# Split FFN and output weights kept in DRAM for the second half of the tokens, with a six-tile chunk between the halves

## The chip, the cores and the metric

The kernel runs on one core of one Trainium2 chip. The metric is the device time of one execution in microseconds: the median of three runs. The core has five engines that work side by side, each through its own list of instructions in order: TensorE (PE) for matmuls, VectorE (DVE), ScalarE (ACT), GpSimd (POOL) and SyncE (SP). SyncE and GpSimd issue DMAs here.

## The reference

Two layers of a trunk on 1152 tokens (1024 of a sample, 128 of a prompt) of width 1024. Each layer is a normalization, an input projection, four mixers, an output projection `w_out` with a gated residual, and then a SwiGLU feed-forward network (FFN) of width 2816 with a gated residual:

```
h = rmsnorm(x) * (1 + scale) + shift
x = x + gate * ((silu(h @ w1) * (h @ w3)) @ w2)
```

All inputs and outputs are float32. The change touches `w_out`, `w1`, `w3` and the order of the FFN.

## The kernel before

A float32 matmul is done as three matmuls of a reduced float32 type: each operand is split into a high part (a rounded copy) and a low part (what is left), and high x high, high x low and low x high are summed in PSUM (`mm3`). Splitting a weight costs one cast on ScalarE and one subtract on VectorE (`wsplit` for `w_out` and `w2`, `wstr` for `w1` and `w3`). Split weights stand in two pools of buffers: the tag `ws` with two buffers, and a pool of 19 large buffers that also holds the activations; raw weights of `wsplit` have one buffer (`wr`).

The tokens are worked on in two halves of 576, each as two quarters of 288. The input side of the FFN, per tile of 128 hidden columns of `w1` and `w3` (22 tiles, index `f`), uses a scheme of seven products in place of eight: `wstr` forms seven split combinations of the four 128x512 pieces of the raw weights (7 casts, 7 subtracts and 4 adds or subtracts of raw pieces), in four buffers; the products are 12 matmuls each, 84 a tile, and VectorE and ScalarE add them up and apply the silu (`ffn_in`). The output side (`ffn_out`) multiplies the hidden tiles of a chunk by `w2`, 48 matmuls a hidden tile and half. Chunks are 2, 4, 4, 4, 4, 4 hidden tiles: an input stage of so many tiles, then an output stage, whose results are added to `x` at once (line 1569, `resid`).

The order of the instructions is written out by generators. `fill_add` queues items, each a pair of `pre` (load and split the weights) and `run` (the matmuls, with a yield after each product). `pre` of the next item is issued after the first yield of the current one. Each layer runs `out_half` (the output projection, eight items for each half), then for both halves all chunks. Beside it `prep(l, 0)` and `prep(l, 1)` make the normalized input of either half (seven buffers `A`) on VectorE and ScalarE; that of half 1 needs the buffers of half 0 and runs around the last output stage of half 0. In layer 0 a generator `side` computes the modulation of layer 1 on VectorE from 24 loads of 1 MB (`wm`, issued by SyncE), stepped three times per hidden tile in both halves.

All weight loads are issued by SyncE, in program order: a load that waits for its buffer holds back those behind it.

Of the kernel before, what the change touches and what calls it, by code (L numbers as in the profile page):

```python
# [21 lines left out]
KT = 8  # L22
# [8 lines left out]
CHUNKS = (2, 4, 4, 4, 4, 4)  # L31
# [249 lines left out]
class Trunk:  # L281
# [10 lines left out]

    SUM = staticmethod(lambda nc: nc.vector)
# [1358 lines left out]
    def layer(s, l, st):  # L1652
# [115 lines left out]
        for p in range(2):  # L1768
            t0 = 0
            sc = []  # L1770
            for ci, nh in enumerate(CHUNKS):
                last = ci == len(CHUNKS) - 1
# [7 lines left out]
        e = len(CHUNKS) - 1  # L1780
# [18 lines left out]
    def out_half(s, l, m, h, mh, ev):  # L1799

        def pre():
# [16 lines left out]
    def wstr(s, l, f):  # L1818

        nc = s.nc  # L1820
        r = s.d("raw")[:, :2048].rearrange("p (x h n) -> p x h n", x=2, h=2)
# [4 lines left out]
        tile_ = [s.d2("ws", F32R, w=1024) if i % 2 else s.t("ws", (128, 2, 1024), F32R, bufs=s.b_ws) for i in range(4)]  # L1826
        B = [None] * 7

        def add(out, a, b, op):
            s.SUM(nc).tensor_tensor(out=out, in0=a, in1=b, op=op)  # L1830

        def part(i, at, src):
            t = tile_[at // 2][:, at % 2]
            hi, lo = t[:, :512], t[:, 512:]
            nc.scalar.copy(hi, src)  # L1835
            nc.vector.tensor_tensor(out=lo, in0=src, in1=hi.bitcast(F32), op=ALU.subtract)  # L1836
            B[i] = (hi, lo)
        part(0, 0, b11)
        add(t3, b22, b12, ALU.subtract)
        add(b12, b12, b11, ALU.subtract)  # L1840
        part(2, 2, b12)
        add(b12, b12, b22, ALU.subtract)
        part(1, 1, b12)
        part(3, 3, b21)
        part(4, 4, t3)
        part(5, 5, b22)
        add(b21, b21, b12, ALU.add)
        part(6, 6, b21)
        return B

    def ffn_in(s, l, p, f, A, hid, sc, side):
# [3 lines left out]
        def pre():  # L1855
            return s.wstr(l, f)

        def run(B):
# [19 lines left out]
            def add(out, a, b, e=nc.vector):  # L1878
                e.tensor_tensor(out=out, in0=a, in1=b, op=ALU.add)  # L1879
# [11 lines left out]
            next(side, None)  # L1891
            nc.scalar.copy(p5, prod(2, "m"))
# [4 lines left out]
            next(side, None)  # L1897
            add(c21, prod(4, "m"), c12)
            add(c22, c21, p5, s.SUM(nc))
            add(c12, c12, p5, s.SUM(nc))  # L1900
# [3 lines left out]
            yield 1580  # L1904
# [214 lines left out]
```

## Time and profile before

| | us |
|---|---|
| median of three runs | 3399.97 |
| lowest and highest | 3396.93, 3400.04 |
| the profiled execution, its own time | 3406.3 |
| its span in the trace | 3404.5 |
| TensorE busy | 3222.8 (95%) |
| VectorE busy | 2613.6 (77%) |
| ScalarE busy | 1436.5 (42%) |
| GpSimd busy | 27.9 (1%) |

The profile is of one execution. Busy time is the time in which an engine had an instruction in work; a share of the span is a mean over stages that differ. The mean granted clock of TensorE over the span is 0.974 of full speed. "Idle before" an instruction, with an arrow to a name, is the time its engine stood still and what ended that. Matmuls are pipelined, so their modelled ends overlap the next by a little.

### The profile page before, as it was taken

Reading aid. Unit: us, or ns where it says so; the run is one execution under the profiler, and the core shown is the slowest. Engines: PE = TensorE matmul, PEld = TensorE weight load, DVE = VectorE, ACT = ScalarE, POOL = GpSimd, SP = SyncE. Lnnn points to the kernel's source line nnn. Section 1 sums busy time; section 2 is a strip of 40 time slices with the busy share of each in tenths; the row PEclk is TensorE's granted clock in tenths of the full one; section 3 lists DMA queues with packets and bytes.
Section 4 is the critical chain, followed back from the end, with each engine's and each line's share of the span. In section 5 each row is a group of like instructions: output and inputs, shape, how many; then the busy total and the mean of one; then the engine's idle time right before and its main releaser. Section 6 shows DMA issues by size and latency. Waiting matters only on the chain. (4 is left out here: it accounts for less than half of the span.)

```text
span 3404.5 us, 64037 instructions
## 1 busy us (share of the span) xinstructions
PE 3222.8 (95%) x26412; PEld 2961.8 (87%) x26412; DVE 2613.6 (77%) x5458; ACT 1436.5 (42%) x2737; POOL 27.9 (1%) x101
## 2 busy tenths in 40 slices
PE   7999999999899999799999999999989999889998
PEld 3657878899889999699998887889889999889998
DVE  6735876558789999999988687655778877988877
ACT  5437254333433443434444635433344434534433
POOL 0000000000000000000000000000000000000000
PEclk8999999999999999899999999999999999989999
DMA  7441101233233333233323110113322232222322
GB/s 275 174 152 31 50 16 34 67 123 132 81 113 124 113 129 100 81 116 121 124 80 107 33 50 17 33 67 127 134 81 82 94 100 81 72 93 94 100 81 72
DMA packets 103889, 319.26 MB, mean 94 GB/s; under 512 B 16496, under 2 KB 33766, under 8 KB 91821
## 3 DMA queue, kind: packets, MB, share of 16 engines
q1 hardware_dynamic: 101692, 300.82, 26.5%
q0 software_dynamic: 1904, 14.35, 1.2%
q8 instruction: 208, 3.41, 0.4%
q14 instruction: 85, 0.69, 0.1%
HBM read 285.58 MB, written 29.56 MB: 93 GB/s over the span
## 5 line engine op out<-in xcount | busy, mean ns | idle before, releaser
L303 PE MATMUL pm<-u,ws 128*128 128x384 f32 x3456 | 680.4, 348 | 14.3 <-DVE ws L347 5.4
L303 PE MATMUL pm<-A,ws 128*128 128x288 f32 x4224 | 631.4, 299 | 28.9 <-ACT ws L1835 7.8
L303 PEld LDWEIGHTS pm<-u,ws 128*128 128x128 f32 x3456 | 603.2, 191 | 42.8 <-issue 8.5
L303 PEld LDWEIGHTS pm<-A,ws 128*128 128x128 f32 x4224 | 587.3, 191 | 39.5 <-ACT ws L1835 8.6
L303 PE MATMUL ps<-hid,ws 128*128 128x288 f32 x4224 | 584.6, 298 | 14.2 <-DVE sc L1879 6.0
L303 PEld LDWEIGHTS ps<-hid,ws 128*128 128x128 f32 x4224 | 570.0, 190 | 23.7 <-DVE sc L1879 7.3
L303 PE MATMUL ps<-A,ws 128*128 128x288 f32 x3168 | 484.3, 301 | 27.6 <-ACT ws L1835 22.1
L303 PEld LDWEIGHTS ps<-A,ws 128*128 128x128 f32 x3168 | 445.5, 192 | 36.1 <-ACT ws L1835 25.3
L1835 ACT CAST ws<-raw 128x512 fp32r<-128x512 f32 x528 | 318.7, 619 | 335.2 <-DVE raw L1830 159.8
L1836 DVE TENSOR_TENSOR ws<-raw,ws 128x512 fp32r<-128x512 f32 x528 | 353.2, 684 | 21.7 <-ACT ws L1835 20.1
L346 ACT CAST ws<-wr 128x1024 fp32r<-128x1024 f32 (+2 forms) x186 | 187.0, 1005 | 269.7 <-DMA wr<-w 94.2
L347 DVE TENSOR_TENSOR ws<-wr,ws 128x1024 fp32r<-128x1024 f32 (+2 forms) x186 | 216.6, 1165 | 98.9 <-ACT ws L346 97.4
L1569 DVE SCALAR_TENSOR_TENSOR x<-ps,mod,x 128x288 f32<-128x288 f32 (+2 forms) x480 | 206.3, 451 | 81.6 <-PE ps L303 79.7
L303 PE MATMUL pm<-mh,ws 128*128 128x288 f32 x1536 | 218.9, 303 | 17.8 <-DVE x L1569 11.4
L303 PEld LDWEIGHTS pm<-mh,ws 128*128 128x128 f32 x1536 | 211.9, 194 | 22.6 <-issue 12.2
L1830 DVE TENSOR_TENSOR raw<-raw 128x512 f32<-128x512 f32 x264 | 180.7, 684 | 2.6
L475 DVE SCALAR_TENSOR_TENSOR acc<-wm,cT,acc 128x512 f32<-128x512 f32 x168 | 121.2, 743 | 0.0
L303 PEld LDWEIGHTS pm<-ws,u 128*128 128x128 f32 x864 | 107.5, 188 | 9.4 <-issue 3.8
L303 PE MATMUL pm<-ws,u 128*128 128x272 f32 (+1 forms) x864 | 114.9, 289 | 0.5 <-DVE lr L879 0.4
L1884 ACT CAST hid<-sc 128x288 fp32r<-128x288 f32 x176 | 75.2, 432 | 77.9 <-DVE sc L1883 77.2
L749 DVE COPY_PREDICATED DS<-masks,ps 128x320 f32<-128x320 uint8 x192 | 89.1, 477 | 21.6 <-PE ps L303 21.4
L1879 DVE TENSOR_TENSOR sc<-ps,p 128x288 f32<-128x288 f32 x176 | 79.5, 452 | 33.0 <-PE ps L303 27.6
(331 smaller groups left out, 3815.9 us busy)
## 6 DMA issues: line engine op xcount, KB each, us to landing
raw<-w SPq DMA_DIRECT2D x176, 512.0 KB, 4.5
wm<-w_mod SPq DMA_DIRECT2D x48, 1024.0 KB, 6.5
wr<-w SPq DMA_DIRECT2D x80, 512.0 KB, 3.7
wr<-w_in SPq DMA_DIRECT2D x48, 512.0 KB, 3.5
wr<-w_out SPq DMA_DIRECT2D x32, 512.0 KB, 3.6
dft<-dft_s POOLq DMA_DIRECT2D x12, 1152.0 KB, 5.6
xscr<-x SPq DMA_DIRECT2D x8, 1152.0 KB, 6.6
x<-xscr SPq DMA_DIRECT2D x8, 1152.0 KB, 5.4
```

Of the source, the lines that this page charges most:

```text
L303: return s.nc.tensor.matmul(out, lhsT, rhs, start=start, stop=stop)
L346: nc.scalar.copy(w[:, 0, :n], raw[:, :n])
L347: nc.vector.tensor_tensor(out=w[:, 1, :n], in0=raw[:, :n], in1=w[:, 0, :n].bitcast(F32), op=ALU.subtract)
L475: nc.vector.scalar_tensor_tensor(out=acc[:, x], in0=wk, scalar=cc, in1=acc[:, x], op0=ALU.mult, op1=ALU.add)
L749: nc.vector.copy_predicated(Dt[g][:, j], s.masks[:, li].unsqueeze(1).to_broadcast([128, nb, 64]), ps[j])
L1569: nc.vector.scalar_tensor_tensor(out=x[k][:, a:b], in0=ps[:, a - g * QT:b - g * QT], scalar=gcol[:, k, st:st + 1], in1=x[k][:, a:b], op0=A ...
L1830: s.SUM(nc).tensor_tensor(out=out, in0=a, in1=b, op=op)
L1835: nc.scalar.copy(hi, src)
L1836: nc.vector.tensor_tensor(out=lo, in0=src, in1=hi.bitcast(F32), op=ALU.subtract)
L1879: e.tensor_tensor(out=out, in0=a, in1=b, op=ALU.add)
L1884: nc.scalar.copy(hi, a)
```

## The change

In half 0 the four buffers of split `w1` and `w3` of each tile are written to a DRAM tensor (`wscr`) by SyncE once they are split: three of 1 MB and one of 512 KB, of which the fourth holds one combination. In half 1 they are loaded from there by GpSimd, with no raw load, cast or subtract. The same is done with the split `w_out`: written by SyncE in half 0 (`oscr`), loaded by GpSimd in half 1. The chunks are 4, 4, 4, 4, 6 in half 0 and 6, 4, 4, 4, 4 in half 1; the output stage of a chunk of six takes its `w2` in eight pieces of 768 columns and not four of 1024. The modulation is stepped in half 1 only, six times per tile. The output projection uses the PSUM buffers `s` (four) in place of `m` (two). A parameter that chose the engine of some adds goes; it was VectorE everywhere.

```diff
-CHUNKS = (2, 4, 4, 4, 4, 4)
+CHUNKS = ((4, 4, 4, 4, 6), (6, 4, 4, 4, 4))
...
-            for ci, nh in enumerate(CHUNKS):
+            for ci, nh in enumerate(CHUNKS[p]):
...
-                s.fill_add([s.ffn_in(l, p, f, A[p], hid, sc, side) for f in range(t0, t0 + nh)], ("in", l, p, ci))
+                s.fill_add([s.ffn_in(l, p, f, A[p], hid, sc, side if p else iter(())) for f in range(t0, t0 + nh)], ("in", l, p, ci))
...
-                    s.fill_add([s.ffn_out(l, p, t0, nh, hid, m, evf(last)) for m in range(0, KT, 2)], ("w2", l, p, ci))
+                    n = 1 if nh > 4 else 2
+                    s.fill_add([s.ffn_out(l, p, t0, nh, hid, m, n, evf(last)) for m in range(0, KT, n)], ("w2", l, p, ci))
...
         def pre():
-            return s.wsplit(s.A["w_out"][l, m].rearrange("p k n -> p (k n)"))
+            if h:
+                w = s.t("ws", (128, 2, 1024), F32R, bufs=s.b_ws)
+                nc.gpsimd.dma_start(w, s.oscr[l][m])
+            else:
+                w = s.wsplit(s.A["w_out"][l, m].rearrange("p k n -> p (k n)"))
+                nc.sync.dma_start(s.oscr[l][m], w.bitcast(F32))
+            return w
...
-                ps = s.p("m")[:, :QT]
+                ps = s.p("s")[:, :QT]
...
-    def wstr(s, l, f):
+    def wstr(s, l, p, f):
...
+        tile_ = [s.d2("ws", F32R, w=1024) if i % 2 else s.t("ws", (128, 2, 1024), F32R, bufs=s.b_ws) for i in range(4)]
+        B = [(t[:, :512], t[:, 512:]) for t in (tile_[at // 2][:, at % 2] for at in (0, 1, 2, 3, 4, 5, 6))]
+        kept = [(t if i < 3 else t[:, :1], s.wscr[l][f, i] if i < 3 else s.wscr[l][f, i, :, :1]) for i, t in enumerate(tile_)]
+        if p:
+            for t, m in kept:
+                nc.gpsimd.dma_start(t, m)
+            return B
         r = s.d("raw")[:, :2048].rearrange("p (x h n) -> p x h n", x=2, h=2)
...
+        for t, m in kept:
+            nc.sync.dma_start(m, t.bitcast(F32))
         return B
...
             yield 1580
             next(side, None)
+            next(side, None)
             nc.scalar.copy(p5, prod(2, "m"))
...
-            add(c22, c21, p5, s.SUM(nc))
-            add(c12, c12, p5, s.SUM(nc))
+            add(c22, c21, p5)
+            add(c12, c12, p5)
...
-            for m in range(2):
+            for m in range(n):
...
+                s.wscr.append(dr.tile([NFF, 4, 128, 2, 1024], F32, name=f"wscr{l}"))
+                s.oscr.append(dr.tile([KT, 128, 2, 1024], F32, name=f"oscr{l}"))
```

On SyncE, in half 0 of layer 0, at a place inside a chunk, the order before was this (`raw` are the loads of `w1` and `w3`, `wr` of `w2`, `wm` of the modulation; "x2" stands for the two loads of one tile, `w1` and `w3`):

```order
L344 DMA wr_11765<-w 128x2x512
L1823 DMA raw_11325<-w 128x1024 x2
L1823 DMA raw_11467<-w 128x1024 x2
L424 DMA wm_11509<-w_mod 128x2048
L1823 DMA raw_11612<-w 128x1024 x2
L424 DMA wm_11685<-w_mod 128x2048
L1823 DMA raw_12068<-w 128x1024
L344 DMA wr_11885<-w 128x2x512
```

and after the change it is this (`wscr` are the writes of the split buffers `ws`):

```order
L1861 DMA wscr_70<-ws_10019 128x2048
L1861 DMA wscr_70<-ws_10018 128x2048
L1861 DMA wscr_70<-ws_10021 128x1024
L1861 DMA wscr_70<-ws_10020 128x2048
L1838 DMA raw_10162<-w 128x1024 x2
L1861 DMA wscr_70<-ws_10160 128x2048
L1861 DMA wscr_70<-ws_10159 128x2048
L1861 DMA wscr_70<-ws_10158 128x2048
L1861 DMA wscr_70<-ws_10161 128x1024
L1838 DMA raw_10303<-w 128x1024 x2
L1861 DMA wscr_70<-ws_10301 128x2048
```

Before, raw loads of consecutive tiles follow one another with only other loads between them. Now the four writes of one tile's split buffers stand ahead of the raw loads of the next.

On ScalarE, at such a place, the order before was this (casts of `raw` are the splits of the next tile, the copies of `pm` take products 2 and 0 out of PSUM, line 1892 the former and line 1887 the latter):

```order
L1835 CAST ws_10788<-raw_10784 128x512
L1835 CAST ws_10789<-raw_10784 128x512
L1835 CAST ws_10790<-raw_10784 128x512
L1892 COPY p_1354_10769<-pm_10826 128x288
L1835 CAST ws_10790<-t_1357_10787 128x512
L1835 CAST ws_10789<-raw_10784 128x512
L1835 CAST ws_10788<-raw_10784 128x512
L1835 CAST ws_10791<-raw_10784 128x512
L1887 COPY p_1368_10910<-pm_10912 128x288
```

and after the change it is this (lines 1847, 1906 and 1900 are the same operations):

```order
L1847 CAST ws_10158<-raw_10162 128x512
L1847 CAST ws_10159<-raw_10162 128x512
L1847 CAST ws_10160<-raw_10162 128x512
L1906 COPY p_1263_10143<-pm_10202 128x288
L1847 CAST ws_10160<-t_1270_10165 128x512
L1847 CAST ws_10159<-raw_10162 128x512
L1900 COPY p_1278_10283<-pm_10285 128x288
L1847 CAST ws_10158<-raw_10162 128x512
L1847 CAST ws_10161<-raw_10162 128x512
```

The copy of product 2 stands behind three casts of the next tile's raw weights in both; the copy of product 0 has moved ahead of two casts. On VectorE the splits stand at like places. On GpSimd, which issued almost nothing in this part before, the loads of half 1 stand in an order given by when their buffers come free: at the change of halves the loads of the first two tiles are mixed, and the third buffer of the first tile comes behind a load of the second tile whose buffer is one that the preparation of half 1 used.

## Rows read from the trace of the kernel before

**Rows 1.** The page: busy us, share of the span and instructions by engine.

```profile
PE 3222.8 (95%) x26412; PEld 2961.8 (87%) x26412; DVE 2613.6 (77%) x5458; ACT 1436.5 (42%) x2737; POOL 27.9 (1%) x101
```

**Rows 2.** Windows: length; PE, PEld, DVE, ACT, POOL busy; PEclk; DMA share, GB/s: one chunk.

```profile
2677.80:2722.60 44.80, 44.80 (x340) 44.80 (x339) 41.66 (x81) 24.09 (x48) 0.00 (x0) 1.00 0.25 83
2722.50:2748.10 25.60, 25.60 (x195) 25.56 (x193) 15.55 (x29) 5.73 (x9) 0.00 (x0) 1.00 0.33 103
```

**Rows 3.** Windows: FFN, layers 0 and 1: half 0, change, half 1.

```profile
950.40:1345.50 395.10, 378.98 (x2828) 369.35 (x2827) 361.51 (x687) 158.51 (x308) 0.00 (x0) 0.99 0.36 119
1345.50:1497.80 152.30, 124.07 (x846) 115.64 (x845) 142.63 (x336) 66.16 (x147) 0.00 (x0) 0.91 0.28 92
1497.70:1819.40 321.70, 316.92 (x2395) 310.79 (x2393) 293.39 (x612) 134.56 (x257) 0.33 (x6) 1.00 0.33 109
2565.00:2932.80 367.80, 364.84 (x2728) 362.98 (x2727) 306.85 (x613) 159.41 (x305) 0.00 (x0) 1.00 0.27 88
2932.80:3080.50 147.70, 127.52 (x822) 120.13 (x821) 131.82 (x320) 67.12 (x146) 0.00 (x0) 0.88 0.27 88
3080.40:3389.10 308.70, 307.89 (x2315) 306.63 (x2313) 252.57 (x523) 127.31 (x243) 0.00 (x0) 1.00 0.27 85
```

**Rows 4.** Groups of instructions, VectorE, layer 1 half 0.

```profile
L1836 DVE TENSOR_TENSOR ws<-raw,ws 128x512 fp32r<-128x512 f32 x121 | 80.9, 684 | 4.5 <-ACT ws L1835 3.7
```

**Rows 5.** Groups of instructions, ScalarE, same stretch.

```profile
L1835 ACT CAST ws<-raw 128x512 fp32r<-128x512 f32 x120 | 72.5, 619 | 76.9 <-PE ps L303 45.1 <-DVE raw L1830 30.6 <-PE pm L303 0.2
```

**Rows 6.** Timeline (start, length, engine): one run of splits, layer 0.

```profile
1331.13 1.28 DVE L1836 TENSOR_TENSOR ws<-raw,ws 128x512 fp32r<-128x512 f32 x2
...
1334.14 0.68 DVE L1836 TENSOR_TENSOR ws<-t,ws 128x512 fp32r<-128x512 f32 x1
1335.11 0.68 DVE L1836 TENSOR_TENSOR ws<-raw,ws 128x512 fp32r<-128x512 f32 x1
...
1337.65 0.68 DVE L1836 TENSOR_TENSOR ws<-raw,ws 128x512 fp32r<-128x512 f32 x1
...
1338.62 0.68 DVE L1836 TENSOR_TENSOR ws<-raw,ws 128x512 fp32r<-128x512 f32 x1
```

**Rows 7.** Timeline: raw weights issued and first used, layer 1.

```profile
2754.54 0.81 SPq L1823 DMA_DIRECT2D raw<-w  x2
...
2762.06 1.14 ACT L1835 CAST ws<-raw 128x512 fp32r<-128x512 f32 x2
```

**Rows 8.** The page: DMA issues, KB each, median us from issue to landing.

```profile
raw<-w SPq DMA_DIRECT2D x176, 512.0 KB, 4.5
wr<-w SPq DMA_DIRECT2D x80, 512.0 KB, 3.7
dft<-dft_s POOLq DMA_DIRECT2D x12, 1152.0 KB, 5.6
```

**Rows 9.** Windows: a stretch where the DMA engines are full.

```profile
15.00:60.00 45.00, 32.94 (x230) 17.42 (x228) 32.35 (x63) 25.72 (x51) 0.00 (x0) 0.80 1.01 424
```

**Rows 10.** Timeline of TensorE at the change of halves, layer 1.

```profile
2963.41 3.13 PE L303 MATMUL ps<-hid,ws 128*128 128x288 f32 x12 [4.02 <-DVE x L1569]
```

**Rows 11.** Timeline of VectorE there: first and last preparation step.

```profile
2944.98 0.38 DVE L625 SCALAR_TENSOR_TENSOR ut<-x,G,pa 128x160 f32<-128x160 f32 x1
...
2988.53 0.46 DVE L615 TENSOR_TENSOR A<-ut,A 128x288 fp32r<-128x288 f32 x1 [1.89 <-ACT A L614]
```

**Rows 12.** Windows: output projection, layer 0.

```profile
828.50:950.60 122.10, 111.70 (x792) 108.38 (x791) 83.39 (x192) 45.56 (x89) 0.00 (x0) 0.96 0.28 91
```

**Rows 13.** Timeline in the output projection, half 0: one weight tile.

```profile
862.40 12.42 SPq L344 DMA_DIRECT2D wr<-w_out  x3
...
867.24 1.23 DVE L347 TENSOR_TENSOR ws<-wr,ws 128x1024 fp32r<-128x1024 f32 x1 [2.81 <-ACT ws L346]
```

**Rows 14.** Windows: two loads that GpSimd issues, and their transfer.

```profile
755.00:757.00 2.00, 2.00 (x14) 2.00 (x13) 0.00 (x0) 0.10 (x1) 1.06 (x2) 1.00 0.91 346
759.00:765.00 6.00, 6.00 (x53) 6.00 (x53) 5.97 (x10) 1.25 (x2) 0.00 (x0) 1.00 1.05 408
```

More of the change, by code (lines that the diff above doesn't have):

```diff
@@ L291 @@
     AH = 3
-    SUM = staticmethod(lambda nc: nc.vector)
     VP, VB = (2, 3, 3), ((1, 2), (0,))
@@ L1770, in layer @@
             sc = []
-            for ci, nh in enumerate(CHUNKS):
-                last = ci == len(CHUNKS) - 1
+            for ci, nh in enumerate(CHUNKS[p]):
+                last = ci == len(CHUNKS[p]) - 1
                 hid = []
-                s.fill_add([s.ffn_in(l, p, f, A[p], hid, sc, side) for f in range(t0, t0 + nh)], ("in", l, p, ci))
+                s.fill_add([s.ffn_in(l, p, f, A[p], hid, sc, side if p else iter(())) for f in range(t0, t0 + nh)], ("in", l, p, ci))
                 if last and p:
@@ L1825, in wstr, with part @@
         t3 = s.tmp("t3")
-        tile_ = [s.d2("ws", F32R, w=1024) if i % 2 else s.t("ws", (128, 2, 1024), F32R, bufs=s.b_ws) for i in range(4)]
-        B = [None] * 7
         def add(out, a, b, op):
[L1830 to L1834, printed above, removed]
+            nc.vector.tensor_tensor(out=out, in0=a, in1=b, op=op)
+        def part(i, src):
+            hi, lo = B[i]
             nc.scalar.copy(hi, src)
             nc.vector.tensor_tensor(out=lo, in0=src, in1=hi.bitcast(F32), op=ALU.subtract)
-            B[i] = (hi, lo)
-        part(0, 0, b11)
+        part(0, b11)
         add(t3, b22, b12, ALU.subtract)
         add(b12, b12, b11, ALU.subtract)
-        part(2, 2, b12)
+        part(2, b12)
         add(b12, b12, b22, ALU.subtract)
[L1843 to L1846, printed above, removed]
+        part(1, b12)
+        part(3, b21)
+        part(4, t3)
+        part(5, b22)
         add(b21, b21, b12, ALU.add)
-        part(6, 6, b21)
+        part(6, b21)
+        for t, m in kept:
+            nc.sync.dma_start(m, t.bitcast(F32))
         return B
@@ L1855, in pre @@
         def pre():
-            return s.wstr(l, f)
+            return s.wstr(l, p, f)
         def run(B):
@@ L1876, in prod, with add @@
                 return ps
-            def add(out, a, b, e=nc.vector):
-                e.tensor_tensor(out=out, in0=a, in1=b, op=ALU.add)
+            def add(out, a, b):
+                nc.vector.tensor_tensor(out=out, in0=a, in1=b, op=ALU.add)
             def hidden(hi, lo, a, b):
@@ L1897, in run @@
             next(side, None)
+            next(side, None)
             add(c21, prod(4, "m"), c12)
-            add(c22, c21, p5, s.SUM(nc))
-            add(c12, c12, p5, s.SUM(nc))
+            add(c22, c21, p5)
+            add(c12, c12, p5)
             yield 1580
@@ L1904, in run @@
             yield 1580
+            next(side, None)
             next(side, None)
@@ L1920, in w2_tile, with ffn_out @@
         return ps
-    def ffn_out(s, l, p, t0, nk, hid, m0, ev):
+    def ffn_out(s, l, p, t0, nk, hid, m0, n, ev):
         def pre():
-            return s.w2_split(l, m0, 2, t0, nk)
+            return s.w2_split(l, m0, n, t0, nk)
         def run(w):
-            for m in range(2):
+            for m in range(n):
                 for q in range(2):
@@ L2009, in main @@
             s.dp, s.gp, s.ps = dp, gp, ps
-            s.hscr, s.hnyq, s.xscr, s.mscr = {}, {}, [], []
+            s.hscr, s.hnyq, s.xscr, s.mscr, s.wscr, s.oscr = {}, {}, [], [], [], []
             for l in range(DEPTH):
```

3 lines of the change are left out of this document (2 added, 1 removed).

## The prediction

> **What bounds the kernel now.** I read the page first: TensorE is busy for 95% of the span [rows 1], so a gain must come from its idle time or from time at the lower clock. Next a window on one chunk of four tiles in layer 1: products 44.80 us, output tiles 25.60 us, TensorE busy throughout at full clock [rows 2]. That is 336 and 192 matmuls, 0.1333 us each, and I take it as the floor (11.2 us a tile of the input stage). Then the FFN in windows of its stages [rows 3], each less its floor:
> - layer 0: half 0 up to its last output stage has 2712 matmuls, floor 361.6, took 395.1: 33.5 lost. The change of halves (792, 105.6) took 152.3: 46.7 lost. The rest of half 1 (2304, 307.2) took 321.7: 14.5 lost.
> - layer 1: 367.8, 147.7 and 308.7: 6.2, 42.1 and 1.5 lost.
>
> So layer 1 has nothing to win but at the change of halves. The sharpest sign there is a wait of 4.02 us on VectorE's line 1569 [rows 10], and the granted clock of the whole stretch is 0.88, against 1.00 on both sides [rows 3].
>
> **The change, half 0: raw weights behind writes.** This is the largest term and it is a loss. Of one tile's splits each cast takes 0.62 us on ScalarE [rows 5], each subtract 0.68 on VectorE [rows 4]; the run I timed lasted from 1331.13 to 1339.30, 8.1 us of a tile's 11.2, and its four buffers were complete 4.5, 3.5, 1.0 and 0 us ahead of its end [rows 6]. They are unchanged. Before, the raw weights of the next tile were issued at 2754.54 and first used at 2762.06, 7.5 us later [rows 7], against a median landing of 4.5 [rows 8]: 3 us to spare. Now SyncE issues four writes, each waiting for a split, and only then the next raw load. Queued behind the waiting writes are thus the raw loads and the output weights, and for these ScalarE, VectorE and TensorE wait.
>
> Of each tile 3.67 million bytes are written. In a stretch where the DMA engines are full they move 424 GB/s [rows 9]: 1.05 million bytes take 2.5 us. The first buffer ready at -4.5, the four transfers end near +4.2, with about 1 us for issue +5.4. The raw pair (1.05 million bytes behind them) is whole near +8 to +9. One cast (0.7) and 8.1 us of splits follow: a period of 16.7 us where TensorE needs 11.2. In a chunk of four, tiles one and two are prepared under the output stage and the first products, and the third tile's raw data, due about 20 us into the stage, comes at about 19. The fourth's is due near 20 to 22 on ScalarE, because the casts stand in its order ahead of copies that free PSUM for the third tile's late products; it comes at 24.7. Estimated loss per chunk: 5.1, plus 1.3 on such copies even where the data is in time, plus 2 at the lower clock behind the wait (an estimate, far below the 18 us that a clock of 0.88 costs in 147.7 us at the change of halves [rows 3], where waits follow one another): 8.4. The chunk of six has three late tiles (5.1, 5.7, 5.7) and 3.3 of the rest: 20. So half 0 loses 4 x 8.4 + 20 = 53 us in either layer. Bounds: 25 if raw data lands within 4.5 us in spite of the writes (1.3 for each tile and the wait of the six), 65 if the writes to DRAM also stall the output stages' loads. I take 53, since the ceiling row is measured and the order of SyncE is fixed. Against before: layer 1 +47, layer 0 +20 (there the modulation's VectorE work leaves half 0, but the raw weights end last).
>
> **Change of halves.** Before, the new half's preparation ran from inside the last output stage (it starts 2932.8) to 2988.99 [rows 11], 55.7 us; in that time stood one tile's splits, 11 x 0.6 = 6.8, which go. The output stage of six tiles covers 288 x 0.1333 = 38.4, perhaps 43, since its eight weight loads come one after another (0.5 + 3.7 of landing + about 1 for the cast = 5.2 against 4.8 us). Preparation is late next: it ends at +49.5, and one load of the first tile is queued on GpSimd behind one that waits for it, +7 (such a load of 1152 KB lands 5.6 after its issue [rows 8], and two issues stand ahead); 3 products, 4.8, remain: +62, where 38.4 + 11.2 = 49.6 is the floor. With the clock's share some 15 is lost, 18 in layer 0. That gives 15 - 42.1 = -27 and 18 - 46.7 = -29, each +-8.
>
> **Half 1.** Its 22 tiles per layer have neither casts nor subtracts, but TensorE was at the floor already: nothing to win in layer 1. I count 1 us a chunk for loads that wait for a buffer and 2 for the chunk of six: +6. In layer 0 the modulation (24 loads of 1.05 million bytes, line 424) now all falls into half 1, about one a tile: with 3.67 million bytes, 4.7 in 11.2 us, 420 GB/s, which is the ceiling [rows 9], and loads for the output stages stand behind it on SyncE. I take +13 between 0 (all hidden; VectorE is relieved of 11 x 0.6 us a tile) and +40.
>
> **Output projection.** It took 122.1 where 768 matmuls need 102.4 [rows 12]. A load is issued at 862.40, when the split before ends, and the next split starts at 867.24, ends 868.47: 6.1 us a tile, against 6.4 of matmuls [rows 13]. A write of 1.05 million bytes ahead of each load makes it 8.5: 2.1 x 5 items, less slack, +7 in half 0. Half 1 loses its splits and has four PSUM buffers: -10 of about 15 lost there. -3 a layer (+-7). The split of w_out needs no more room, since the buffers are the same.
>
> **Sum.** Layer 0: 20 - 29 + 13 - 3 = +1. Layer 1: 47 - 27 + 6 - 3 = +23. Together +24 on the profiled execution's 3406.3 (span 3404.5): 3430. The median of the runs shown, 3399.97, is 6.3 below that execution, so 3424.
>
> **A rule to weigh: loads issued by GpSimd.** Two such loads cost it 0.53 us each, and were issued while VectorE was busy for 0.00 of 2.00 us; during their transfer VectorE was busy for 5.97 of 6.00 and the DMA engines moved 408 GB/s [rows 14]. So the transfer isn't hurt, and the issue beside a busy VectorE isn't shown. The Trainium skill ("SBUF — State Buffer", the warning on DVE blocking DMA) says that GpSimd writes the descriptors of its DMAs itself and can be locked out meanwhile by VectorE; no run here shows it. By that rule half 1 would go as in the third rival below.
>
> **Rivals.**
> 1. The writes hide: raw data comes in time, half 0 falls to 25 in each layer or to the floor. For it: the mean DMA share in half 0 is 0.27 to 0.36 [rows 3], so bytes as such have room. Against it: the order on SyncE. It decides if the raw pair lands within some 5 us of the last split. Then layer 1 has +19, layer 0 -9: 2 x 28 = 56 less, 3368; with half 0 at its floor up to 40 less again, 3328. This is faster than before.
> 2. It evens out: half 0 at 40 each, 26 less, 3398, or the change of halves gains 8 more in each layer.
> 3. Loads of half 1 come late, by GpSimd's issue or by the modulation. For it: VectorE and DMA are full in layer 0. Against it: one tile's four issues need 4 x 0.53 = 2.1 of 11.2 us. If each issue waits for one subtract of 0.68 [rows 4], a tile comes up to 2.7 us late; half of that and all of it on 44 tiles is +59 and +119, less the +19 counted: 3464 to 3524.
>
> **How the numbers follow.** The forecast has 0.43, the first rival 0.32, the second 0.14, the third 0.11. A measurement of this kernel can tell 0.2%, 6.8 us, from no change. Faster holds the first rival and a part of the second: 0.35; the same 0.12; slower the forecast and the third: 0.53. The forecast's own range, half 0 between 45 and 60 and the other terms by their bounds, is 3403 to 3452. The range for all, 3345 to 3462, leaves out one in ten at either end.
>
> **What would show it.** In the windows of layer 1: half 0 longer by about 47, the change of halves shorter by 27. On the timeline: raw loads issued right behind the fourth write, landing 8 us after the last split, and casts idle for them; at the change of halves no 4 us wait on line 1569. I am wrong if half 0 in layer 1 stays within 20 us of its floor, or if half 1 loses more than 30 in a layer.

## The result, and the profile after

The kernel got slower: 3537.18 us (median of four runs, 3529.22 to 3542.13) against 3400.01 before, a ratio of 1.0396 with an interval of 1.0367 to 1.0425. The forecast was 3424, range 3345 to 3462. Its sign was right and its size far off: +24 on the profiled execution, where the span went from 3404.5 to 3537.3, +132.8.

The windows of the changed kernel answer to [rows 3] and [rows 12]: the output projection of layer 0, then for each layer half 0 up to its last output stage, that output stage of six tiles, and half 1. The columns are those of [rows 2].

```profile
832.50:952.80 120.30, 109.91 (x791) 106.73 (x790) 73.95 (x183) 38.18 (x81) 4.24 (x8) 0.97 0.52 178
952.70:1383.30 430.60, 384.24 (x2632) 374.92 (x2631) 300.91 (x592) 158.98 (x300) 0.00 (x0) 0.92 0.69 259
1383.30:1444.40 61.10, 47.57 (x296) 44.03 (x295) 47.43 (x116) 27.70 (x66) 2.65 (x5) 0.89 0.37 121
1444.40:1889.70 445.30, 415.74 (x3140) 401.01 (x3138) 304.75 (x643) 91.60 (x192) 44.64 (x89) 0.98 0.73 261
2633.90:3062.80 428.90, 380.61 (x2633) 370.29 (x2632) 300.53 (x592) 159.39 (x300) 0.00 (x0) 0.92 0.69 260
3062.80:3126.40 63.60, 49.49 (x301) 46.28 (x299) 47.39 (x117) 27.60 (x66) 2.65 (x5) 0.87 0.35 116
3126.40:3522.40 396.00, 391.80 (x2932) 388.09 (x2931) 197.75 (x467) 84.39 (x174) 44.00 (x83) 1.00 0.67 231
```

Less the floor of 0.1333 us a matmul (348.8, 38.4 and 387.2 us; 102.4 for the output projection):

| us lost | before | forecast | measured |
|---|---|---|---|
| half 0, layer 0 | 33.5 | 53 | 81.8 |
| half 0, layer 1 | 6.2 | 53 | 80.1 |
| change of halves, layer 0 | 46.7 | 18 | 22.7 |
| change of halves, layer 1 | 42.1 | 15 | 25.2 |
| half 1, layer 0 | 14.5 | 27.5 | 58.1 |
| half 1, layer 1 | 1.5 | 7.5 | 8.8 |
| output projection, layer 0 | 19.7 | 16.7 | 17.9 |

The columns do not cover the same stretches. "Before" is the prediction's split of the old chunks, with its own floors. The forecast's 18 and 15 for the change of halves include the wait of the first tile of half 1, while the measured 22.7 and 25.2 are the output stage of six alone; the input stage of six behind it loses 11.4 more in layer 0 and 2.7 in layer 1, which stand in the rows of half 1.

In layer 1, half 0 was near its floor before and now waits, as the forecast had it. The windows show that VectorE is less busy there (300 us of 429, 307 of 368 before), while the DMA share went from 0.27 to 0.69 and the granted clock from 1.00 to 0.92.

The page of the changed kernel names the wait. Its groups show what ended idle time, its issues the median time to landing (4.5 us for `raw` before [rows 8]):

```profile
L301 PE MATMUL pm<-A,ws 128*128 128x288 f32 x4224 | 663.8, 308 | 93.1 <-ACT p L1906 58.5
...
L1847 ACT CAST ws<-raw 128x512 fp32r<-128x512 f32 x264 | 159.4, 619 | 260.9 <-DMA raw<-w 105.5
...
wscr<-ws SPq DMA_DIRECT2D x132, 1024.0 KB, 3.9
...
raw<-w SPq DMA_DIRECT2D x88, 512.0 KB, 7.0
```

Copies out of PSUM (line 1906, product 2) release TensorE, and they stand behind casts that wait for the raw weights. The timeline of SyncE in the first chunk of layer 1 shows why the weights are late; a merged row spans several issues:

```profile
2634.48 5.00 SPq L1861 DMA_DIRECT2D wscr<-ws  x4
2639.58 2.49 SPq L1838 DMA_DIRECT2D raw<-w  x2
2655.31 4.67 SPq L1861 DMA_DIRECT2D wscr<-ws  x4
2660.07 2.71 SPq L1838 DMA_DIRECT2D raw<-w  x2
2674.57 5.13 SPq L1861 DMA_DIRECT2D wscr<-ws  x4
2679.79 2.43 SPq L1838 DMA_DIRECT2D raw<-w  x2
```

Each pair of raw loads is issued 0.1 us behind the fourth write. The pairs start 20.5 and 19.7 us apart, where TensorE needs 11.2. On ScalarE and on TensorE in that chunk:

```profile
2670.19 1.83 ACT L1847 CAST ws<-raw 128x512 fp32r<-128x512 f32 x3 [2.18 <-DMA raw<-w]
...
2688.30 1.86 ACT L1847 CAST ws<-raw 128x512 fp32r<-128x512 f32 x3 [6.67 <-DMA raw<-w]
```

```profile
2690.51 3.25 PE L301 MATMUL pm<-A,ws 128*128 128x288 f32 x12 [5.08 <-ACT p L1906]
```

The raw weights issued at 2679.79 are first cast at 2688.30, after 6.67 us of idleness; the copy behind those casts lets TensorE go on at 2690.51, after 5.08 us. That is the very step that [rows 7] stood for before. The 12 matmuls behind this wait then take 3.25 us, twice their floor of 1.6, and the window on them has a granted clock of 0.50, the lower of TensorE's two levels (1.2 GHz):

```profile
2690.50:2693.80 3.30, 3.25 (x12) 2.90 (x12) 3.30 (x7) 1.25 (x3) 0.00 (x0) 0.50 0.10 40
```

The waits of SyncE itself over half 0 of layer 1 (total us, times, longest) show that it stood at its writes for the splits:

```profile
SPq L1861 <- DVE ws L1848: 249.3, 73, 13.2
```

At the change of halves the wait of [rows 10] did not go; it went into the output stage of six tiles. TensorE, then VectorE:

```profile
3099.80 0.53 PE L301 MATMUL ps<-hid,ws 128*128 128x288 f32 x2 [3.24 <-DVE x L1567]
3101.09 6.05 PE L301 MATMUL ps<-hid,ws 128*128 128x288 f32 x34 [0.76 <-DVE ws L345]
3109.41 0.53 PE L301 MATMUL ps<-hid,ws 128*128 128x288 f32 x2 [2.26 <-DVE x L1567]
3110.70 6.30 PE L301 MATMUL ps<-hid,ws 128*128 128x288 f32 x34 [0.76 <-DVE ws L345]
3118.91 0.53 PE L301 MATMUL ps<-hid,ws 128*128 128x288 f32 x2 [1.92 <-DVE x L1567]
```

```profile
3100.09 0.95 DVE L345 TENSOR_TENSOR ws<-wr,ws 128x768 fp32r<-128x768 f32 x1
...
3101.69 2.03 DVE L623 SCALAR_TENSOR_TENSOR ut<-x,G,pa 128x160 f32<-128x160 f32 x6
...
3108.47 0.46 DVE L613 TENSOR_TENSOR A<-ut,A 128x288 fp32r<-128x288 f32 x1
3108.84 0.94 DVE L1567 SCALAR_TENSOR_TENSOR x<-ps,mod,x 128x288 f32<-128x288 f32 x2
3109.69 0.95 DVE L345 TENSOR_TENSOR ws<-wr,ws 128x768 fp32r<-128x768 f32 x1
```

Each split of a `w2` piece (line 345) and each addition of results (line 1567) stands behind a slice of the new half's preparation, 7 us from 3101.69 to 3108.84. TensorE waits 2 to 3 us for each, and the 34 matmuls after such a wait take 6.0 to 6.3 us where 4.5 is the floor.

In half 1 of layer 0, last, the DMA engines are nearly full in the input stage of six. Over the whole half GpSimd's loads waited 63 us for buffers that the modulation's VectorE steps hold, and TensorE itself 18.8 us for split weights from DRAM (in the second view: total us, times, longest):

```profile
1444.40:1523.00 78.60, 72.16 (x560) 68.98 (x559) 60.03 (x120) 16.06 (x39) 10.07 (x19) 1.00 0.91 339
```

```profile
POOL ws L1834 <- DVE acc L473: 63.0, 9, 18.1
...
PE pm L301 <- DMA ws<-wscr: 18.8, 11, 4.2
```

The floor of this half leaves out the modulation's own matmuls on TensorE. There are 216 of them here, busy for 14.3 us; before, half of them stood in half 0.

### The profile page after: what moved, and what is told of

Read it like the earlier page. It is cut to its first block, busy times and chain, and to the rows that moved or that the text cites. A ratio compares the mean times of both kernels' runs of the same rounds, so it can differ in the third digit from the quotient of the medians.

```text
span 3537.3 us, 63966 instructions
## 1 busy us (share of the span) xinstructions
PE 3270.1 (92%) x26412; PEld 2999.1 (85%) x26412; DVE 2305.7 (65%) x4878; ACT 1258.1 (36%) x2413; POOL 130.2 (4%) x293
## 5 line engine op out<-in xcount | busy, mean ns | idle before, releaser
L301 PE MATMUL pm<-A,ws 128*128 128x288 f32 x4224 | 663.8, 308 | 93.1 <-ACT p L1906 58.5
L301 PEld LDWEIGHTS pm<-A,ws 128*128 128x128 f32 x4224 | 611.9, 198 | 111.4 <-ACT p L1906 62.2
L301 PEld LDWEIGHTS ps<-A,ws 128*128 128x128 f32 x3168 | 452.6, 195 | 11.8 <-ACT ws L1847 10.1
L344 ACT CAST ws<-wr 128x1024 fp32r<-128x1024 f32 (+3 forms) x170 | 170.1, 1000 | 302.5 <-DMA wr<-w 165.2
L345 DVE TENSOR_TENSOR ws<-wr,ws 128x1024 fp32r<-128x1024 f32 (+3 forms) x170 | 197.4, 1161 | 107.9 <-ACT ws L344 106.1
L1847 ACT CAST ws<-raw 128x512 fp32r<-128x512 f32 x264 | 159.4, 619 | 260.9 <-DMA raw<-w 105.5
L301 PE MATMUL ps<-mh,ws 128*128 128x288 f32 x1536 | 216.6, 301 | 21.6 <-ACT ws L344 11.0
L1848 DVE TENSOR_TENSOR ws<-raw,ws 128x512 fp32r<-128x512 f32 x264 | 177.0, 687 | 89.4 <-ACT ws L1847 87.5
L301 PEld LDWEIGHTS ps<-mh,ws 128*128 128x128 f32 x1536 | 209.1, 192 | 27.0 <-ACT ws L344 12.9
L1892 DVE TENSOR_TENSOR sc<-ps,p 128x288 f32<-128x288 f32 x176 | 80.1, 455 | 165.5 <-PE ps L301 158.4
L1834 POOL DMA_DIRECT2D ws<-wscr x176 | 93.6, 534 | 1676.2 <-PE ps L301 588.6
L1892 DVE TENSOR_TENSOR sc<-pm,sc 128x288 f32<-128x288 f32 x176 | 79.8, 453 | 67.8 <-PE pm L301 67.8
```

What stands on the lines that cost most here:

```text
L301: return s.nc.tensor.matmul(out, lhsT, rhs, start=start, stop=stop)
L344: nc.scalar.copy(w[:, 0, :n], raw[:, :n])
L345: nc.vector.tensor_tensor(out=w[:, 1, :n], in0=raw[:, :n], in1=w[:, 0, :n].bitcast(F32), op=ALU.subtract)
L1834: nc.gpsimd.dma_start(t, m)
L1892: nc.vector.tensor_tensor(out=out, in0=a, in1=b, op=ALU.add)
```

## The experiments

What a stage "loses" is its time in the profiled execution less its floor; "half 0" is up to its last output stage. A kernel's time is the median of its runs; e2 to e7, v2, v3 and x4 are one run each. Each edit is made to the changed kernel if nothing else is said.

**Where the writes stand.** There are two theories for half 0: the place of the raw loads behind the writes on SyncE (theory 1), or the bytes that are written. The first run moves the writes to another engine.

```diff
-            nc.sync.dma_start(m, t.bitcast(F32))
+            nc.gpsimd.dma_start(m, t.bitcast(F32))
```

> The changed kernel, with the writes of the split w1 and w3 in half 0 issued by GpSimd in place of SyncE; the bytes are the same. Theory 1 (order on SyncE: the raw loads stand behind four writes that wait for the splits): half 0 of layer 1 up to its last output stage goes from 429 us (floor 348.8) to 350-365 us, likewise in layer 0, and the whole kernel to about 3390-3420. Rival (the written bytes themselves fill the DMA engines or the memory, whoever issues them): half 0 stays above 410 us and the kernel above 3500.

```profile
2591.20:2982.60 391.40, 365.48 (x2632) 359.56 (x2632) 295.55 (x592) 152.97 (x299) 46.81 (x88) 0.97 0.76 284
```

The kernel takes 3456.18 us, 81 less than the changed one. Half 0 of layer 1 loses 42.6, not 80.1 and not the 1 to 16 of theory 1. The input stages of four tiles are down to 1.6 to 2.3, the first one to 6.8; but the output stages behind them now lose 3.6 to 6.3 each. At one of them:

```profile
2714.28 1.05 ACT L344 CAST ws<-wr 128x1024 fp32r<-128x1024 f32 x1 [2.56 <-DMA wscr<-ws]
...
2722.06 1.04 ACT L344 CAST ws<-wr 128x1024 fp32r<-128x1024 f32 x1 [2.29 <-DMA wr<-w]
...
2723.83 11.39 PE L301 MATMUL ps<-hid,ws 128*128 128x288 f32 x66 [3.54 <-ACT hid L1897]
```

The first `w2` split waited 2.56 us for a write, because one of the two `ws` buffers was not free. The next cast of `w2` then waited for its load, and a hidden tile's cast behind it held TensorE for 3.54 us. That gave theory 2, buffers held by writes, for the rest.

A second run keeps the writes on SyncE and puts them behind the next load of raw weights or of `w2`; nothing else moves by design.

```diff
+    def flush(s):
+        for t, m in s.late:
+            s.nc.sync.dma_start(m, t.bitcast(F32))
+        s.late = []
...
+        if not p:
+            r = s.d("raw")[:, :2048].rearrange("p (x h n) -> p x h n", x=2, h=2)
+            for x, n in enumerate(("w1", "w3")):
+                nc.sync.dma_start(r[:, x].rearrange("p h n -> p (h n)"), s.A[n][l, f].rearrange("p k n -> p (k n)"))
+        s.flush()
...
-        for t, m in kept:
-            nc.sync.dma_start(m, t.bitcast(F32))
+        s.late = kept
```

(The raw loads stood below the allocation of the split buffers. `wsplit` calls `flush` too, behind its load.)

> The changed kernel with the same writes, all still issued by SyncE, but those of one tile are put behind the next load of raw weights (of the next tile, or of w2) and no longer ahead of it. Theory 1 (position on SyncE, not the issuing engine): the input stages of four tiles in half 0 of layer 1 lose 0-3 us each (10 in the changed kernel), the first 5-8 (26), the six 5-9 (22); the output stages may still lose up to 6, as in e1; half 0 of layer 1 375-395, the kernel 3440-3475. Rival (GpSimd's own path made the difference in e1): input stages still lose 8 or more, the kernel above 3510.

```profile
2579.70:2955.70 376.00, 361.32 (x2633) 353.81 (x2632) 297.22 (x592) 155.01 (x300) 0.00 (x0) 0.99 0.80 296
```

```profile
2745.30 1.48 SPq L1838 DMA_DIRECT2D raw<-w  x2
2749.05 11.23 SPq L337 DMA_DIRECT2D wscr<-ws  x4
2760.69 2.69 SPq L1838 DMA_DIRECT2D raw<-w  x2
```

This is the decisive run: 3435.47 us, 102 less than the changed kernel, with the same bytes from the same engine, at 296 GB/s. That is a little under the range expected. Half 0 of layer 1 loses 27.2. The input stages of four tiles lose at most 2.6, the first 11.1 (more than the 5 to 8 expected), the six 8.2, the output stages 1 to 1.8. Raw pairs are 15 us apart, and the writes of the tile before still stand between them; what changed is that a raw load no longer waits for the splits of the tile just ahead of it. So the place on SyncE is shown as the main cause, 53 of the 80 us; GpSimd's path is not needed to explain e1's gain. Of the 27 left, 4.3 stay without any writes (e4 below); what makes up the rest was not tried by itself.

**Held buffers.** Two runs write only some of the buffers (base: e1): the second and fourth (the diff), or `kept[::2]`, the first and third.

```diff
-        for t, m in kept:
+        for t, m in kept[1::2]:
             nc.gpsimd.dma_start(m, t.bitcast(F32))
```

> The kernel with the writes by GpSimd (e1), but of each tile only the second and fourth buffer are written, those from the pool of 19 (1.57 of 3.67 million bytes); half 1 loads the same bytes as before, from the written places, so its numbers aren't the reference's. Theory 2 (a write holds its buffer until it has landed; the first w2 split of an output stage needs one of the two ws buffers and so waits for the last writes): the output stages of four tiles in half 0 of layer 1, which lose 4 to 6 us each with all writes, lose 0 to 1. Rival (the bytes as such slow them): the loss falls with the bytes, to 1.5-3.

```profile
2555.50:2910.50 355.00, 350.53 (x2632) 348.61 (x2631) 295.67 (x593) 155.41 (x301) 23.40 (x44) 1.00 0.53 184
```

> As the run before, but only the first and third buffer of each tile are written, those from the tag with two buffers (2.1 of 3.67 million bytes); half 1 loads from the written places, so its numbers aren't the reference's. Theory 2: the output stages of four tiles in half 0 of layer 1 still lose 4 to 6 us each. Rival (bytes): 2.3-3.5.

```profile
2561.80:2939.40 377.60, 360.62 (x2633) 356.62 (x2632) 296.14 (x592) 156.34 (x300) 23.39 (x44) 0.98 0.55 203
```

With the pool's buffers alone, output stages lose 0 to 1.5 and half 0 6.2 in all; with the `ws` buffers alone 0.3, 5.3, 5.7 and 4.8, 28.8 in all. The loss goes with the buffer, not with the bytes (1.57 against 2.1 million a tile), as theory 2 had it. But x1 writes the same `ws` buffers and its output stages lose 1 to 1.8 us; why writes by SyncE hold them at less cost is open.

Then all four buffers were taken from the pool, with writes by GpSimd (v1), in the last tile of a chunk only (v2), and with writes by SyncE (v3).

```diff
-        tile_ = [s.d2("ws", F32R, w=1024) if i % 2 else s.t(...) for i in range(4)]
+        tile_ = [s.d2("ws", F32R, w=1024) if i % 2 or not p else s.t(...) for i in range(4)]
```

> All four buffers of a tile are written in half 0 and by GpSimd (as in e1), but in half 0 all four come from the pool of 19, none from the tag with two ws buffers, so no w2 split waits for a write. Theories 1 and 2 together: half 0 of layer 1 up to its last output stage comes within 3-10 us of its floor of 348.8 (392 in e1, 429 in the changed kernel), and the kernel to 3385-3405. Rival (bytes, which e5 had cut to 1.57 of 3.67 million): half 0 still loses 20 or more, the kernel above 3415.

The expectation failed: 3563.2 us, slower than the changed kernel. The waits of SyncE in half 0 of layer 1:

```profile
SPq L1838 <- DMA wscr<-ws: 86.0, 5, 18.2
SPq L1838 <- DVE ws L1848: 74.7, 10, 12.8
```

The raw loads (line 1838) come from the same pool of 19 and now wait for buffers that the writes and splits hold. The edit moved the held buffer and did not remove it.

> As v1, but only the last tile of each chunk in half 0 has all its buffers from the pool; the others have two from the ws tag. Theory 2 (only the w2 split behind a chunk's last tile meets a write that hasn't landed): the output stages of four tiles in half 0 of layer 1 lose 0 to 1 us, as in v1; the kernel 3385-3410. Rival (the ws buffers hold up the next tile's splits inside the chunk as well): the input stages lose 2-4 us each more than in v1.

3460.43 us, as e1 and above the range. Output stages lose 2.3 to 4.3, input stages of four 2.8 to 3.7: half of each theory, so inconclusive.

> As v1, but the writes are issued by SyncE, as in the changed kernel: no w2 split waits for a write, but the raw loads stand behind the writes again. Theory 1 (order, by itself): the input stages of four tiles in half 0 of layer 1 lose 8-11 us each again, the first one 25 and the six 20, the output stages 0-1; half 0 415-430, the kernel 3500-3530. Rival (the held ws buffers were what made the raw order matter): input stages lose 3 or less each.

3559.54 us, above the range. The output stages of four lose 0.0, as theory 2 says, and the input stages 11 to 12, the first 26.3, the six 29.8; since the pool runs short here too, it does not separate place from pool.

A fourth run, v4, is v1 with the modulation stepped in both halves. It was expected at 3375 to 3400 us, with 20 to 30 lost in each half of layer 0; the rival was that the loss only moves from half 1 to half 0, with the kernel within 8 us of v1 or above it. It took 3573.93 us. Half 1 of layer 0 lost 21.5, as expected, but half 0 lost 145, where v1 lost 100: the rival's way.

The last run on buffers writes those of e5 by SyncE:

> As e5 (only the second and fourth buffer of a tile are written, 1.57 of 3.67 million bytes; half 1 loads from the written places, so its numbers aren't the reference's), with these writes issued by SyncE, ahead of the next raw loads. Theory 1: the next raw load still waits for the end of the splits, so the input stages lose again, but less, as 2.1 million bytes fewer stand ahead of it (5 us at 424 GB/s): 2-6 us per stage of four in layer 1, where e5 lost none; the first 12-20. Rival (bytes ahead of the load matter, not its place): 0-1, as in e5.

3418.03 us; half 0 of layer 1 loses 10.9, the input stages of four nothing, the first 8.4. Theory 1's 2 to 6, and 12 to 20 for the first, were not seen. One difference is in SyncE's order: mostly one of the two raw loads now stood ahead of the tile's last write, and the other behind it.

```profile
2746.89 0.37 SPq L1838 DMA_DIRECT2D raw<-w  x1
2749.72 0.33 SPq L1861 DMA_DIRECT2D wscr<-ws  x1
2750.10 0.48 SPq L1838 DMA_DIRECT2D raw<-w  x1
```

So writes by SyncE ahead of raw loads can be nearly free. That the place costs by itself, without the bytes of all four writes ahead of the load, is not shown: x1 changed the place with all bytes there, and x4 has both fewer bytes and a partly changed order.

**Modulation.**

```diff
-  s.ffn_in(l, p, f, A[p], hid, sc, side if p else iter(()))
+  s.ffn_in(l, p, f, A[p], hid, sc, side)
```

(One `next(side, None)` stands in place of each two.)

> The changed kernel, with the modulation of the next layer stepped three times per tile in both halves, as before the change. Theory (in half 1 of layer 0 the 24 modulation loads of 1 MB beside 3.67 million bytes per tile fill the DMA engines and their VectorE work holds buffers): half 1 of layer 0 falls from 445 us (floor 387) to 405-425, half 0 of layer 0 rises by 5-15 from 431; the kernel 3510-3530. Rival (half 1 of layer 0 is slow for the loads from DRAM alone): half 1 stays above 435.

Half 0, then the change of halves with half 1, of layer 0:

```profile
946.30:1423.10 476.80, 399.80 (x2740) 382.15 (x2739) 361.01 (x702) 159.33 (x305) 0.00 (x0) 0.90 0.71 264
1423.10:1897.80 474.70, 447.90 (x3326) 438.98 (x3324) 292.18 (x651) 118.25 (x252) 47.20 (x94) 0.98 0.67 229
```

3551.99 us. Half 1 without the change loses 24.6 in place of 58.1, as expected; half 0 rises by 46, not by 5 to 15. The same modulation costs more where raw weights are late already, so the kernel is no faster for it.

**Chunks.** Old chunks, and new chunks without DRAM:

```diff
-CHUNKS = ((4, 4, 4, 4, 6), (6, 4, 4, 4, 4))
+CHUNKS = ((2, 4, 4, 4, 4, 4), (2, 4, 4, 4, 4, 4))
```

> The changed kernel, with chunks of 2, 4, 4, 4, 4, 4 tiles in both halves. Theory (the output stage of six tiles is no cover: its eight small w2 pieces are split behind slices of the preparation on VectorE): the stretch from the last output stage of half 0 to the end of half 1 in layer 1, 459.6 us now (floor 425.6 for it), falls relative to its floor from 34 to about 20-25, and half 0 loses 10-20 less as no chunk has six late tiles: kernel 3480-3510. Rival (six tiles do cover, and the loss is the preparation's in any case): the change of halves loses 34 or more and the kernel stays at 3530-3560.

3541.83 us, no better: the rival held, in its numbers. The change of halves with half 1 of layer 1 lost 40, against 34 with the new chunks, and half 0 76, against 80. The old chunks also start half 1 with two tiles and not six, so this run does not tell what the six ahead of the change are worth.

```diff
-        if p:
+        if p and f < 0:
...
-        for t, m in kept:
+        for t, m in kept if f < 0 else []:
```

> The changed kernel without any keeping in DRAM: weights are split anew in half 1, as before; the new chunks, the modulation in half 1 and the PSUM buffers of the output projection stay. Theory 1: half 0 of layer 1 returns to 352-360 us (floor 348.8); the change of halves still loses 30-50 in either layer; half 1 of layer 0 loses 30-60 (three things on VectorE); the kernel 3400-3440. Rival (chunks, not DRAM, make half 0 slow): half 0 of layer 1 stays above 400.

(The `w_out` part is undone too.) The change of halves with half 1 of layer 0, then half 0 and the same rest of layer 1:

```profile
1305.80:1856.50 550.70, 478.59 (x3432) 455.91 (x3432) 492.79 (x1001) 204.79 (x411) 0.33 (x6) 0.95 0.35 119
2601.50:2954.60 353.10, 349.99 (x2632) 348.45 (x2632) 296.40 (x593) 156.09 (x301) 0.00 (x0) 1.00 0.27 87
2954.60:3421.00 466.40, 444.33 (x3229) 437.30 (x3228) 380.69 (x822) 196.26 (x392) 0.00 (x0) 0.97 0.27 88
```

3438.62 us. Half 0 of layer 1 is back at 4.3 over its floor, so chunks do not make it slow. The rest of layer 1 loses 40.8, as before the change (43.6); that of layer 0 125, more than expected. There splits, preparation and a doubled modulation meet on VectorE, which is busy for 493 of 551 us. The third run on chunks puts the six before the last (base: e1).

```diff
-CHUNKS = ((4, 4, 4, 4, 6), (6, 4, 4, 4, 4))
+CHUNKS = ((4, 4, 4, 6, 4), (6, 4, 4, 4, 4))
```

> The kernel with the writes by GpSimd (e1), with chunks 4, 4, 4, 6, 4 in half 0 and 6, 4, 4, 4, 4 in half 1, so that the output stage at the change of halves has four tiles in four pieces of w2. Theory 3 (with eight pieces, each split stands on VectorE behind a slice of the preparation, so TensorE waits for the preparation inside the output stage, and six tiles of work hide no more of it): the last output stage of half 0 and the first input stage of half 1 in layer 1 together lose 30-38 us, against 27.6 with six tiles ahead, as the preparation's time is nearly the same and 12.8 us of cover is gone. Rival (the eight pieces themselves cost the time): together they lose 15 or less.

```profile
2996.10:3446.10 450.00, 431.11 (x3134) 423.01 (x3132) 241.14 (x581) 110.33 (x236) 45.95 (x87) 0.98 0.64 218
```

The window is from the last output stage of half 0 to the end of half 1 (floor 412.8). The kernel takes 3462.79 us. The last output stage and the first input stage of layer 1 together lose 28, where e1 has 27.6: neither 30 to 38 nor 15. So 12.8 us more of cover, in eight small pieces, won nothing here: the preparation is waited for inside the stage or behind it. Whether cover is worth nothing, or the pieces cost beside the preparation what the cover wins, the run does not tell. Away from the preparation the pieces are cheap: in half 1 of layer 1 of the changed kernel the output stage of six loses 1.1 us.

**Parts, and a version that beats both.** New chunks, `w_out` kept, modulation in both halves, nothing of `w1` and `w3` kept (e8); then the first six (x2) or three tiles (x3, the diff) kept, written by GpSimd. The modulation is as in e2.

```diff
-        if p:
+        if p and f < 3:
...
-        for t, m in kept:
-            nc.sync.dma_start(m, t.bitcast(F32))
+        for t, m in kept if f < 3 else []:
+            nc.gpsimd.dma_start(m, t.bitcast(F32))
```

> The changed kernel with w1 and w3 split anew in half 1 (nothing of them in DRAM) and the modulation in both halves, three steps a tile; the new chunks and the w_out kept in DRAM stay. Theory: with neither writes in the FFN nor the modulation packed into half 1, the FFN of layer 0 takes 865-880 us (937 in the changed kernel, 869 before), that of layer 1 815-825 (824 before), the output projections 117-121; the kernel is 3385-3410, no slower than before. Rival (the six-tile chunks cost time by themselves): 3415 or more.

3400.82 us. Its ratio to the kernel before is 0.9999 (interval 0.9989 to 1.0009): no difference.

> As e8 (new chunks, modulation in both halves, w_out kept), and the split w1 and w3 of the first six tiles alone are kept in DRAM, written by GpSimd. Theory: at the change of halves the six tiles come without splits, so that layer 1 loses 26-30 there and not 38, layer 0 26-32 and not 45; the first chunk of half 0 loses 4-8 more for its writes; the kernel 3375-3395, under both kernels. Rival (what the writes cost in half 0 eats what the change of halves wins): 3395-3415.

3398.49 us, 0.9991 (0.9977 to 1.0004). The change of halves fell as expected (26.3 lost in layer 1 with the output stage and the six), but half 0 of layer 0 lost 15 more than in e8: the rival's way.

> As x2 with three tiles kept, none of them the last of a chunk. Theory: the first chunk's output stage loses nothing, and at the change of halves the tiles that meet the preparation are the first ones, so nearly all of the gain stays: 3375-3395, within 5 us of x2. Rival (all six have to be free of splits): 3390-3405, between e8 and x2.

Half 0 and the rest of layer 1:

```profile
2563.30:2920.20 356.90, 353.40 (x2633) 351.58 (x2631) 296.42 (x593) 155.74 (x301) 6.40 (x12) 0.99 0.34 117
2920.20:3380.00 459.80, 439.88 (x3230) 433.95 (x3228) 362.17 (x789) 184.83 (x371) 6.37 (x12) 0.98 0.33 106
```

3391.06 us, 0.9964 (0.9952 to 0.9977): faster than both kernels. Half 0 of layer 1 loses 8.1, the rest 34.2, with a seventh of the writes. e8 has the same chunks, modulation and `w_out` without the three tiles, so the gain over e8 is theirs.

> As x3 (three tiles kept), with the modulation left out of the first four tiles of half 0 and stepped four times a tile in half 1. Theory (in x3 the first input stage of layer 0 loses 22.6 us against 7.8 in layer 1, because the modulation's loads and VectorE work meet the writes and the start): that stage loses 7-10, half 1 of layer 0 3-8 more than in x3; the kernel 5-12 under x3, 3378-3388. Rival (the start of layer 0 is slow for another reason): no change, 3388-3396.

```diff
-  s.ffn_in(l, p, f, A[p], hid, sc, side)
+  s.ffn_in(l, p, f, A[p], hid, sc, side if p or f > 3 else iter(()))
...
+            if p:
+                next(side, None)
```

3397.64 us, 0.9975 (0.9961 to 0.9988). The first input stage of layer 0 lost 5.7 and not 22.6, as expected, but the rest of that FFN lost 24 more: the modulation's cost moved. The kernel is above both ranges and, against x3, not faster.

> The kernel before the change, with one part of it alone: the split w_out kept in DRAM and loaded by GpSimd for half 1, and the output projection in the PSUM buffers s. The prediction's term was -3 us a layer (+7 for the writes in half 0, -10 for the splits gone in half 1). Theory: the output projections take 116-120 us (122.0 and 121.4 before), the kernel 3388-3399. Rival (the writes ahead of each w_out load cost as much as half 1 saves): 3399-3408.

```profile
828.80:946.00 117.20, 107.34 (x792) 103.91 (x791) 74.19 (x184) 38.02 (x81) 4.24 (x8) 1.00 0.53 184
2437.80:2555.70 117.90, 109.75 (x792) 106.77 (x792) 74.08 (x184) 38.34 (x82) 4.24 (x8) 0.97 0.53 183
```

(Base: the kernel before, with `out_half` and `oscr` of the change.) 3395.63 us, 0.9960 (0.9947 to 0.9974). The output projections take 117.2 and 117.9 us, 4.9 and 3.6 less than before (122.1 and 121.5): the term of -3 a layer was right, and this one part of the change is a gain. It is as large as that of x3 (0.9964), which has this part too. So three kept tiles gain over e8, which has the new chunks, and no run shows that keeping tiles of `w1` and `w3` gains over x6.

## Why the prediction was right or wrong

**Half 0, the largest term: right mechanism, mis-sized.** "Raw weights behind writes" is what the traces show, and x1 shows the place on SyncE as the main cause. The estimate of 53 us measured 82 and 80. Three steps were off; the first two tell largely the same microseconds, by kind and by place.
- The clock. The sum had 2 us a chunk "at the lower clock behind the wait", some 10 in all. In half 0 of layer 1 TensorE was busy for 380.61 us at a granted clock of 0.92; in e4, where it hardly waits, the same matmuls took 349.99 at 1.00. Of these 31 us about 24 are the clock's: by the trace's clock records, 49 us of the busy time lie at a granted 0.50, and half of that is lost. So some 14 of the 27 us missed in layer 1 are in this term. The time that TensorE stood still, 48 us (3 in e4), was nearly that of the sum.
- The first chunk. The step "in a chunk of four, tiles one and two are prepared under the output stage and the first products" does not hold there, since no output stage precedes it. Its first tile's splits ended 5 us into the stage, three tiles were late, and in layer 1 it lost 27.3 with its output stage where 8.4 was put. By chunks this is 19 of the 27.
- The period. It was 18 to 20.5 us, not 16.7. From the issue of a raw pair to its first cast the rows have 10.1 and 8.5 us, where the sum had 8 to 9; from a first cast to the next pair it is 9.6, where the sum had 0.7 + 8.1. The other chunks of four lost 8 to 12 with their output stages, the six 22.

The sum also has a slip: the times of the third and the fourth tile (19 and 24.7) are 5.7 apart, which is not its period, and against a due time of 20 to 22 they do not give 5.1. The 5.5 that a period of 16.7 adds to 11.2 a tile is near it, so the term hardly changes.

**Change of halves: the gain came, less of it.** It was put at 15 and 18 lost and measured 25.2 and 22.7 in the output stage alone, 27.9 and 34.1 with the input stage behind it. The step "preparation is late next", behind an output stage that ends near +43, failed: VectorE's own order put slices of preparation ahead of the last `w2` splits, so the stage itself lasted 63.6 us in layer 1, at a granted clock of 0.87. What stood on VectorE between two splits was to be read from its order before the sum was made. That six tiles are cover was taken for granted, and e7 shows no gain by it. (The preparation's 55.7 us are 56.2 by the two times given; the +49.5 has that right.)

**Half 1 of layer 0: mis-sized.** It was put at 13 on top of 14.5, and 58.1 was lost. By the prediction's own sign (more than 30 lost in a layer's half 1) it was wrong here. The cause that it names, modulation and DRAM loads together, is right: with half of the modulation elsewhere (e2) the loss is 24.6, and in layer 1, with the same loads from DRAM and no modulation, 8.8. I had taken a value near the lower end because VectorE is relieved. But the DMA engines stood at a share of 0.91 in the first window of that half, and TensorE waited 18.8 us for loads. The modulation's own matmuls, 14.3 us of which half moved here, had no term at all.

**Half 1 of layer 1 and the output projection** came near the forecast (8.8 for 7.5; -1.8 and about -1 for -3, and -4.9 and -3.6 with that part alone).

**The rivals.** The first, that the writes hide, did not happen. With the place changed (x1) half 0 of layer 1 loses 27.2, close to the 25 of this rival, so what stood against it, the order on SyncE, was rightly named. The third, late loads in half 1, was right in layer 0 for the modulation's branch. GpSimd's issue was not slow: in half 1 of layer 1 it took 44.0 us for 83 issues, 0.53 each as in [rows 14], beside a VectorE busy for 198 of 396 us, and 8.8 us were lost. The lockout of which the Trainium skill warns ("SBUF — State Buffer", the warning on DVE blocking DMA) is not seen in this stage. The page ties it to VectorE operations in a 2-port mode, a condition that the prediction left out, and no run here shows in which mode these ran.

**The range** failed since three terms came out above their own upper bounds at once: half 0 at 80 to 82 with a bound of 65, the change of halves in layer 1 at 25.2 with 23, half 1 of layer 0 at 58.1 with 54.5. The forecast's sign, slower, rests on half 0, whose mechanism was right, so it is not luck; the size of +24 was a small difference of large terms.

In sum: of the 109 us that the forecast missed, half 0 has 56, half 1 of layer 0 31, the change of halves 15, and the output projection, half 1 of layer 1 and the rest 7.

## What to carry to other kernels

A store that waits for compute should not stand in a queue ahead of the next loads. Put behind them, on the same engine, the same bytes cost a third as much here (27 us for 80). Before keeping something for later, count the buffers that a store holds until it has landed, and who takes them next, and try each part of a change by itself: the kept `w_out` alone (x6) did as well as any version with kept tiles. When a chain of waits gets a new link, work out the first chunk by itself, since nothing runs ahead of it, and give the lower clock behind each wait a term read from rows at either level.

## What the runs showed of the hardware that was not expected

The same DMA bytes from the same engine cost 27 or 80 us of TensorE's time in half 0, by place alone (x1 against the changed kernel), at 296 and 260 GB/s. In half 1 of layer 0 the DMA engines stood at a share of 0.91 with only 339 GB/s in the input stage of six, where in [rows 9] a share of 1.01 went with 424; what makes the loads from DRAM dearer per byte was not tried.

Which engine issues a store mattered by 81 us (e1). The Trainium skill ("DMA: Bandwidth & Descriptors", "Issuing engines are not separate DMA queues") says that issuing from several engines saves only the time that the issue takes on the sequencer. The runs differ: an issue that waits for a split holds those behind it, and with x1 more was won on one engine (102 us).
